# A hybrid S5 / gated-MLP layer: two loads moved to other queues, products with x's low half put last, one stage of the state-space mixer issued a block later

## The chip, the cores and the metric

The kernel runs on one core of a Trainium2 chip. Its engines work side by side, each through a queue of its own: TensorE (PE in the profile, PEld for its weight loads) multiplies, VectorE (DVE), ScalarE (ACT) and GpSimd (POOL) work element by element, and DMA transfers are issued from the queues of SyncE (SP), ScalarE or GpSimd. An engine waits only for the semaphores of its own next instruction. The metric is the device time of one execution in microseconds (us). Less is better.

## The reference

One layer on x of 256 tokens by 2048 columns, all in float32:

```
h   = rmsnorm(x, norm_mix_g)
z   = h @ w_in                          # 2048 -> 3072: [ssm_in 1024 | sgu_u 1024 | sgu_v 1024]
a   = s5(ssm_in), then y * sigmoid(y @ glu_w + glu_b) with y = gelu(s5 output)
b   = gelu(u) * (causal mixing of layernorm(gelu(v)) inside chunks of 128 + bias)
x   = x + concat(rmsnorm(a), rmsnorm(b)) @ w_out          # 2048 -> 2048
x   = x + relu(rmsnorm(x) @ w_up)^2 @ w_down              # 2048 -> 8192 -> 2048
out = rmsnorm(x, norm_final_g)
```

The S5 mixer has 64 groups of 16 channels with 64 complex states each, a diagonal recurrence over the 256 tokens.

## The kernel before

**Two halves for every operand.** A float32 product is made from rounded halves: `split` (line 110) writes the high half with ScalarE and the remainder with VectorE. A product is the sum of three: high weight by high activation, high weight by low activation, low weight by high activation (`which` = 0, 1, 2 in `block_A`). Weights stream through `wparts` (lines 149 to 187): a load of 512 KB on SP's queue brings a pair of row blocks (`raw`, four buffers), and `split` turns it into `whi` and `wlo` (three buffers each).

**Blocks.** `block_A` (line 189) makes 512 output columns with the weights stationary; its activations are `xT`, the transposed x, in a high and a low half. `block_B` (line 242) has the activations stationary and 512 weight columns moving: for each pair, two token halves by two row blocks by three products, 12 in all. The input projection for S5 is two `block_A`s of eight pairs each (lines 798 to 804). Then come the other input projections (`block_B` and `block_A`), the first half of the output projection `wout_half(8, ...)` (four `block_B`s n = 0 to 3 of four pairs, line 988), the GLU (`block_A` with `yhl`, line 1003), the second half of the output projection and the MLP.

**The first block.** x arrives in column blocks of 256 during the first block. `load_x(0)` (line 286) loads the first ones, one token half from SP's queue and one from ScalarE's; the norm's scale `gnat` comes from GpSimd's queue (line 287). `prep_x(i)` (line 347) transposes a column block on TensorE, then ScalarE writes the high half of `xT` with the scale (line 361) and VectorE the low half (line 362). `mids` is a list of seven calls of `prep_x`; a pair of the first block takes one of them in its middle, so that the columns for the next pair are made while this pair is multiplied. The first pair has its own order already (lines 202 to 211); the others take a call after `m == 1`, that is, after 12 of their 24 products.

**Background work.** The S5 mixer is written as generators in the list `bg`; each `yield` names a cost. `pump(d)` (line 117) adds d to a debt and issues pieces until the debt is paid; the blocks call it between their products. `gen_rest` runs the four rounds r = 0 to 3: `gen_f` (states from inputs), `gen_rot` (the recurrence), `gen_lane` (tables for later rounds; with `gen_k` the copies into `Tp` at line 693) and `gen_y` (line 754: 8 products with `Tp`, 16 with `Gp`, which a TensorE profile shows as 16 and 32 passes; then a GELU into `yst`, eight stores to `yd`, and the load of `yT`). `gen_y(r)` runs in round r + 1, and `gen_y(3)` is the last thing in `gen_rest`. The low and high half of `yT` are read by the GLU. `fence(last)` and `behind()` make the next four products of a block stand behind `last` in TensorE's queue. `tc.issue_after(ins)` puts instructions behind another one in the same engine's queue.

The order of each engine's queue is fixed before the run by a scheduler that goes by priority and by what is ready in its own model of time.

Of the kernel before, what the change touches and what calls it, by code (L numbers as in the profile page):

```python
# [18 lines left out]
P = 128  # L19
# [31 lines left out]
def hybrid_layer_kernel(  # L51
# [6 lines left out]
    nc = tc.nc  # L58
    V, A, T, G = nc.vector, nc.scalar, nc.tensor, nc.gpsimd
# [29 lines left out]
    def acc(shape, name="acc"):  # L89

        acc_pools.append(acc_pools.pop(0))
        return acc_pools[-1].tile(shape, F32, tag="acc", name=nm(name))
# [4 lines left out]
    def sx(shape, name="sx"):  # L97
        return pss_.tile(shape, F32, tag="sx", name=nm(name))

    def sq2k(shape, tag, bufs, name=None):  # L100
        return sp.tile(shape, F32, tag=tag, bufs=bufs, name=nm(name or tag))
# [11 lines left out]
    bg = []  # L113
# [3 lines left out]
    def pump(d):  # L117

        debt[0] += d
        while bg and debt[0] > 0:  # L120
            try:
                with tc.high_priority(offset=0):
                    c = next(bg[0])
                debt[0] -= c[0] + 0.4 * c[1] + 1 * c[2]
            except StopIteration:
                bg.pop(0)

    def drain_bg():
        while bg:
            pump(1e9)  # L130
# [3 lines left out]
    def fence(ins):  # L134

        fences[:] = [ins.ins] * 4

    def behind():
        return tc.issue_after(fences.pop()) if fences else nullcontext()


    KS = 2
    stream = {"pool": wp1, "fine": True, "kd": 2, "raw": 4, "d": 0.0}
# [3 lines left out]
    mids = []  # L147
# [41 lines left out]
    def block_A(w, k0, nk, c0, act):  # L189


        banks = [acc([P, 2, S], "accA") for _ in range(2)]
        def product(m, kk, which, kp, hi, lo):
            wt = (hi, hi, lo)[which][:, kk, m * P : m * P + P]
            return T.matmul(  # L195
                banks[m // 2][:, m % 2], wt, act(kp)[which == 1],
                start=(kp == 0 and m % 2 == 0 and which == 0), stop=(kp == nk - 1 and which == 2),
                skip_group_check=True,
            )

        for kp0, hi, lo in wparts(w, k0, nk, c0):
            if kp0 == 0 and len(mids) == 7:

                for kk in range(KS):
                    for which in (0, 2, 1):
                        for m in range(4):
                            last = product(m, kk, which, kk, hi, lo)
                    if kk == 0:
                        mids.pop(0)(last)
                pump(stream["d"])  # L210
                continue
            for m in range(4):
                for kk in range(KS):
                    for which in range(3):
                        with behind() if which == 0 else nullcontext():
                            last = product(m, kk, which, kp0 + kk, hi, lo)
                stream["last"] = last
                if m == 1 and mids:
                    mids.pop(0)(last)
                pump(stream["d"] / 4)  # L220
        return banks
# [40 lines left out]
    gnat = const.tile([16, P], F32, name="gnat")  # L262
# [5 lines left out]
    def load_x(c, engines=(nc.sync, nc.sync)):  # L268
        cs_ = slice(c, c + 256)
        for t in range(2):  # L270
            engines[t].dma_start(xin[t][:, cs_], x[t * P : (t + 1) * P, cs_])
# [11 lines left out]
                nc.sync.dma_start(vnat[r0 : r0 + n, :], v[0].rearrange("(k p) -> k p", p=P))  # L283
            r0 += n

    load_x(0, (nc.sync, nc.scalar))
    nc.gpsimd.dma_start(gnat, norm_mix_g[0].rearrange("(k p) -> k p", p=P))


    ident = const.tile([P, P], F32, name="ident")  # L290
# [120 lines left out]
    Tp = sp.tile([P, RP, 2, 4, 16], F32, name="Tp")  # L411
# [289 lines left out]
    u2, yTs = {}, {}  # L701
# [20 lines left out]
    def gen_f(r):  # L722
        pfs[r] = [sx(sh, "pf") for _ in range(2)]
        for q in range(RP):
            for i in range(2):
                T.matmul(pfs[r][i][:, q], w1s[r][:, i, q], u2[r][:, q], start=True, stop=True)  # L726
            yield 0.0, 0.0, 0.45

    def gen_rot(r):
        cosT, sinT, rhoT = tabs[r]  # L730
        h = [sq2k(sh, "hc", 2) for _ in range(2)]
        yield from cmul(h, cosT, sinT, pfs[r][0], pfs[r][1], sh, ALU.add, ALU.subtract)
        fl = "p q c -> p (q c)"
        for i in range(2):
            V.tensor_tensor_scan(
                h[i].rearrange(fl), rhoT.rearrange(fl), h[i].rearrange(fl), 0.0, ALU.mult, ALU.add
            )
            yield 0.6, 0.0, 0.0

        for i in range(2):  # L740
            t1, t2 = tmp([P, RP, NC4 - 1]), tmp([P, RP, NC4 - 1])
            V.tensor_tensor(t1, h[i][:, :, e63], cosT[:, :, e63], ALU.mult)
            yield 0.6, 0.0, 0.0
            V.tensor_tensor(t2, h[1 - i][:, :, e63], sinT[:, :, e63], ALU.mult)
            yield 0.6, 0.0, 0.0
            for g in range(2):
                gs_ = slice(g * 64, (g + 1) * 64)
                V.tensor_tensor(
                    Eg[i * 64 : (i + 1) * 64, :, g, 1:], t1[gs_], t2[gs_],
                    ALU.subtract if i == 0 else ALU.add,  # L750
                )
                yield 0.6, 0.0, 0.0

    def gen_y(r):
        py = sx(sh, "py")

        for q in range(RP):
            T.matmul(  # L758
                py[:, q], Tp[:, q].rearrange("p g j c -> p (g j c)"), u2[r][:, q],
                start=(q == 0), stop=False, skip_group_check=True,  # L760
            )
            if q % 2 == 1:
                yield 0.0, 0.0, 0.45
        for g in range(2):
            for q in range(RP):
                last = T.matmul(  # L766
                    py[g * 64 : (g + 1) * 64, q], Gp[:, q, g].rearrange("p j c -> p (j c)"), Eg[:, q, g],
                    start=False, stop=True, skip_group_check=True,
                )
        fence(last)  # L770
        yield 0.0, 0.0, 1.6
        yst = sq2k(sh, "zst", 2, "yst")
        A.activation(yst, py, AF.Gelu_apprx_tanh)
        rows_ = yd[r * 256 : (r + 1) * 256]
        for g in range(2):
            for j in range(4):
                p0 = g * 64 + j * 16
                nc.sync.dma_start(
                    rows_[:, j, :].rearrange("(q g p) c -> g p q c", g=2, p=16)[g], yst[p0 : p0 + 16]
                )  # L780
        yTs[r] = sq2k([P, 2, 4, NC4], "uy", 5, "yT")
        nc.sync.dma_start(yTs[r], rows_.rearrange("(m p) j c -> p m j c", p=P))
        yield 0.0, 0.5, 0.0

    def zip_gens(*gens):
        gens = list(gens)
        while gens:
            for g_ in list(gens):
                try:
                    yield next(g_)  # L790
                except StopIteration:
                    gens.remove(g_)
# [5 lines left out]
    for n in range(2):  # L798
        banks = block_A(w_in, 0, 16, n * 512, act_xT)
        with tc.high_priority(offset=AHEAD):  # L800
            if n == 0:
                x_rstd()
            for i, bank in enumerate(banks):
                z_out(n * 2 + i, bank)
# [14 lines left out]
    def gen_out_lane(r):  # L819

        if r > 0:
            yield from gen_y(r - 1)
        yield from gen_lane(r)

    def gen_rest():
        yield from gen_f(0)
        for r in range(4):
            yield from zip_gens(gen_rot(r), gen_out_lane(r))
            if r < 3:
                yield from gen_f(r + 1)  # L830
        yield from gen_y(3)

    bg.append(gen_rest())
    stream["d"] = PACE

# [20 lines left out]
    for n in range(2):  # L856
# [5 lines left out]
        if n == 1:  # L862
# [15 lines left out]
            for side in range(2):  # L878
                for i, half in enumerate(halves[side]):
                    if half is not None:  # L880
                        which = 0 if side == 0 else (1 if i < 3 else 2)
# [25 lines left out]
    def bhl(h):  # L907
        return bfirst[h // 2][:, h % 2] if h < 4 else hls[0][:, 1, h]
# [60 lines left out]
    rsb = const.tile([P, 2], F32, name="rsb")  # L969
# [10 lines left out]
    def wout_half(kt0, act, rs):  # L980
        for n in range(4):
            banks = block_B(w_out, kt0, 8, n * 512, act)
            for t in range(2):
                sl = x2[t][:, n * 512 : (n + 1) * 512]
                V.scalar_tensor_tensor(sl, banks[t], rs[:, t : t + 1], sl, ALU.mult, ALU.add)
            yield n

    for _ in wout_half(8, lambda k: (bhl(k)[:, 0], bhl(k)[:, 1]), rsb):
        pass
    drain_bg()  # L990
    stream["d"] = 0.0

# [9 lines left out]
    for n in range(2):  # L1002
        banks = block_A(glu_w, 0, 8, n * 512, lambda k: (yhl[:, k, 0], yhl[:, k, 1]))
        for i in range(2):
            gt = tmpm([P, 2, 4, NC4], F32, "gt")
            for mm in range(2):
                m = n * 4 + i * 2 + mm
# [6 lines left out]
            for mm in range(2):  # L1014
                m = n * 4 + i * 2 + mm
# [22 lines left out]
    for n in wout_half(0, lambda k: (ahl[k // 4][:, k % 4, 0], ahl[k // 4][:, k % 4, 1]), rsa):  # L1038
# [3 lines left out]
        for k2 in range(2):  # L1042
            pt = sx([P, 2, S], "ptx2")
            for kk in range(2):
                k = n * 4 + k2 * 2 + kk
                for t in range(2):
                    T.transpose(pt[:, kk, t * P : (t + 1) * P], x2[t][:, k * P : (k + 1) * P], ident)
            for kk in range(2):
                k = n * 4 + k2 * 2 + kk
# [148 lines left out]
```

## Time and profile before

| | |
|---|---|
| three runs | 1046.34, 1048.33 (median), 1049.29 us |
| profiled execution | 1048.05 us, span 1046.2 us |
| TensorE busy | 1033.5 us, 99% |
| VectorE busy | 674.3 us, 64% |
| ScalarE busy | 551.1 us, 53% |
| GpSimd busy | 9.3 us, 1% |
| mean granted clock of TensorE | 0.992 |

The span is the time from the first to the last profiled event of one execution. Busy shares are means over stages with different limits, and matmuls are pipelined, so that a busy TensorE is not one at its peak. A granted clock of 1.00 is 2.4 GHz, 0.50 is 1.2 GHz. A few per cent of the matmul records can be missing.

### The profile page before, as it was taken

What the parts mean: (1) busy time and instruction counts of PE and PEld (TensorE: products, weight loads), DVE (VectorE), ACT (ScalarE), POOL (GpSimd) and SP (SyncE); (2) the same over time, 40 slices, a digit from 0 to 9 for tenths busy, and PEclk for the clock granted to TensorE, in tenths of its full rate; (3) what the DMA queues carried; (4) which work ended last, traced back from release to release, by engine and by line L of the source; (5) the groups of instructions that cost most, each with busy time, mean ns of one, the idle gap of its engine ahead of it and who ended that gap; (6) DMA issues with size and microseconds to landing.
All of it is one profiled execution on the core that took longest, in us unless ns stands there. A gap on an engine that the chain in (4) does not pass through costs nothing.

```text
span 1046.2 us, 15091 instructions
## 1 busy us (share of the span) xinstructions
PE 1033.5 (99%) x5865; PEld 896.6 (86%) x5865; DVE 674.3 (64%) x957; ACT 551.1 (53%) x748; POOL 9.3 (1%) x23
## 2 busy tenths in 40 slices
PE   9999999999999999999999999999999999999996
PEld 8998899978988888888888888888888888888886
DVE  7998998765687665544466655456665565655564
ACT  5677658653766555544445543445554334545452
POOL 0100010000000000000000000000000000000000
PEclk9999999989999999999999999999999999999998
DMA  8964555546565666666666666666656566665662
GB/s 280 249 196 129 143 164 159 156 112 214 183 221 161 203 191 190 193 189 199 188 194 186 193 188 196 191 195 183 187 189 191 194 194 191 187 196 185 197 218 85
DMA packets 113047, 195.13 MB, mean 187 GB/s; under 512 B 17864, under 2 KB 23440, under 8 KB 112528
## 3 DMA queue, kind: packets, MB, share of 16 engines
q1 hardware_dynamic: 112112, 193.34, 60.8%
q8 instruction: 46, 0.75, 0.3%
q10 hardware_dynamic: 576, 0.79, 0.2%
q14 instruction: 25, 0.20, 0.1%
q0 software_dynamic: 288, 0.04, 0.0%
HBM read 189.91 MB, written 4.19 MB: 186 GB/s over the span
## 4 chain that ended last, share of the span: by engine, by line
PE 95%; DMA 2%; ACT 1%; DVE 1%; SPq 0%; issue 0%; DVEq 0%
PE accA L235 23%; PE accB L252 15%; PE accB L253 15%; PE accB L254 14%; PE accA L236 11%; PE accA L195 9%; PE pf L726 1%; DMA xin<-in_x_dram 1%; PE py L766 1%; PE py L758 1%; PE accL L1144 1%; PE accL L1143 1%; PE accL L1142 1%; PE pw L621 1%; PE pk L675 1%; PE pm L922 0%
## 5 line engine op out<-in xcount | busy, mean ns | idle before, releaser
L110 DVE TENSOR_TENSOR wlo<-raw,whi 128x1024 fp32r<-128x1024 f32 (+1 forms) x337 | 411.2, 1221 | 329.7 <-ACT whi L110 329.2
L110 ACT ACTIVATE whi<-raw 128x1024 fp32r<-128x1024 f32 (+1 forms) x337 | 356.1, 1059 | 401.3 <-PE accB L254 200.7
L235 PE MATMUL accA<-x2T,whi 128*128 128x512 f32 x1024 | 355.4, 395 | 0.0
L236 PE MATMUL accA<-x2T,wlo 128*128 128x256 f32 x1024 | 280.3, 278 | 0.0
L235 PEld LDWEIGHTS accA<-x2T,whi 128*128 128x128 f32 x1024 | 191.6, 188 | 43.6
L236 PEld LDWEIGHTS accA<-x2T,wlo 128*128 128x128 f32 x1024 | 192.6, 188 | 1.8
L254 PE MATMUL accB<-whi,hT 128*128 128x512 f32 x480 | 186.8, 389 | 0.0
L253 PE MATMUL accB<-wlo,hT 128*128 128x512 f32 x480 | 186.7, 389 | 0.0
L252 PE MATMUL accB<-whi,hT 128*128 128x512 f32 x480 | 167.9, 389 | 0.0
L254 PEld LDWEIGHTS accB<-whi,hT 128*128 128x128 f32 x480 | 90.1, 188 | 18.7
L253 PEld LDWEIGHTS accB<-wlo,hT 128*128 128x128 f32 x480 | 90.1, 188 | 18.6
L252 PEld LDWEIGHTS accB<-whi,hT 128*128 128x128 f32 x480 | 90.0, 188 | 18.6
L195 PE MATMUL accA<-xT,whi 128*128 128x256 f32 x512 | 101.1, 293 | 1.1 <-DVE xT L362 1.1
L195 PEld LDWEIGHTS accA<-xT,whi 128*128 128x128 f32 x512 | 80.2, 191 | 3.1 <-DVE xT L362 2.1
L195 PE MATMUL accA<-xT,wlo 128*128 128x256 f32 x256 | 71.5, 287 | 0.0
L195 PEld LDWEIGHTS accA<-xT,wlo 128*128 128x128 f32 x256 | 48.1, 191 | 0.0
L1096 ACT ACTIVATE cr<-accA 128x256 f32<-128x256 f32 x64 | 24.0, 374 | 7.9 <-PE accA L236 7.9
L253 PE MATMUL accB<-wlo,xT 128*128 128x512 f32 x64 | 25.9, 405 | 0.0
L254 PE MATMUL accB<-whi,xT 128*128 128x512 f32 x64 | 25.2, 394 | 0.0
L252 PE MATMUL accB<-whi,xT 128*128 128x512 f32 x64 | 24.9, 407 | 0.0
L254 PE MATMUL accB<-whi,ahl 128*128 128x512 f32 x64 | 24.8, 393 | 0.0
L253 PE MATMUL accB<-wlo,ahl 128*128 128x512 f32 x64 | 24.8, 393 | 0.0
(291 smaller groups left out, 1026.2 us busy)
## 6 DMA issues: line engine op xcount, KB each, us to landing
raw<-in_w_up_dram SPq DMA_DIRECT2D x128, 512.0 KB, 3.7
raw<-in_w_down_dram SPq DMA_DIRECT2D x128, 512.0 KB, 4.4
raw<-in_w_in_dram SPq DMA_DIRECT2D x47, 512.0 KB, 4.3
raw<-in_w_out_dram SPq DMA_DIRECT2D x32, 512.0 KB, 4.7
raw<-in_ssm_glu_w_dram SPq DMA_DIRECT2D x8, 512.0 KB, 4.3
x<-in_x_dram SPq DMA_DIRECT2D x2, 1024.0 KB, 7.2
xin<-in_x_dram SPq DMA_DIRECT2D x15, 128.0 KB, 4.8
out_dram<-dacc SPq DMA_DIRECT2D x5, 256.0 KB, 4.0
```

Source lines behind the costliest of these rows:

```text
L110: return A.activation(hi, src, AF.Copy), V.tensor_sub(lo, src, hi.bitcast(F32))
L195: return T.matmul(banks[m // 2][:, m % 2], wt, act(kp)[which == 1], start=(kp == 0 and m % 2 == 0 and which == 0), stop=(kp == nk - 1 and ...
L235: T.matmul(o, hi[:, kk, ms], xhl, start=(kp == 0), stop=False, skip_group_check=True)
L236: T.matmul(o[:, 1], lo[:, kk, ms], xhl[:, 0], start=False, stop=(kp == nk - 1), skip_group_check=True,)
L252: T.matmul(banks[t], xh[:, ts_], hi[:, kk], start=(kp == 0), stop=False)
L253: T.matmul(banks[t], xh[:, ts_], lo[:, kk], start=False, stop=False)
L254: stream["last"] = T.matmul(banks[t], xl[:, ts_], hi[:, kk], start=False, stop=(kp == nk - 1))
L621: T.transpose(pw[:, k], Qb[:, i, h2 * 4 + k].rearrange("p e g h -> p (e g h)"), ident)
L675: last = T.matmul(pk[:, q].rearrange("p d c -> p (d c)"), Qb[:, i, q, 0].rearrange("p g h -> p (g h)"), gcs[r][i][:, q, 0:4].rearrange("p ...
L726: T.matmul(pfs[r][i][:, q], w1s[r][:, i, q], u2[r][:, q], start=True, stop=True)
L758: T.matmul(py[:, q], Tp[:, q].rearrange("p g j c -> p (g j c)"), u2[r][:, q], start=(q == 0), stop=False, skip_group_check=True,)
L1096: A.activation(cr[:, mm], b_[:, 1], AF.Copy)
```

## The change

Three things are edited. The first x columns are both loaded from SP's queue, and the norm's scale from ScalarE's. In the first block, the pairs that still have a `prep_x` to place issue the 16 products with the high half of x first, place `prep_x` after the eighth, and issue the eight products with the low half last, calling `pump` there. `gen_y(3)` is taken out of `gen_rest`; after block n = 0 of the output projection's first half the background list is emptied, then `gen_y(3)` is appended to it, and its first products stand behind the last product issued so far.

```diff
@@ block_A @@
                 pump(stream["d"])
                 continue
+            if mids:
+                for kk in range(KS):
+                    for m in range(4):
+                        for which in (0, 2):
+                            last = product(m, kk, which, kp0 + kk, hi, lo)
+                        if kk == 0 and m == 3:
+                            mids.pop(0)(last)
+                for m in range(4):
+                    for kk in range(KS):
+                        last = product(m, kk, 1, kp0 + kk, hi, lo)
+                    stream["last"] = last
+                    pump(stream["d"] / 4)
+                continue
             for m in range(4):
...
-    load_x(0, (nc.sync, nc.scalar))
-    nc.gpsimd.dma_start(gnat, norm_mix_g[0].rearrange("(k p) -> k p", p=P))
+    load_x(0)
+    nc.scalar.dma_start(gnat, norm_mix_g[0].rearrange("(k p) -> k p", p=P))
...
@@ gen_y @@
         for q in range(RP):
-            T.matmul(
-                py[:, q], Tp[:, q].rearrange("p g j c -> p (g j c)"), u2[r][:, q],
-                start=(q == 0), stop=False, skip_group_check=True,
-            )
+            with tc.issue_after(stream["last"].ins) if r == 3 else nullcontext():
+                T.matmul(
+                    py[:, q], Tp[:, q].rearrange("p g j c -> p (g j c)"), u2[r][:, q],
+                    start=(q == 0), stop=False, skip_group_check=True,
+                )
...
@@ gen_rest @@
             if r < 3:
                 yield from gen_f(r + 1)
-        yield from gen_y(3)
...
-    for _ in wout_half(8, lambda k: (bhl(k)[:, 0], bhl(k)[:, 1]), rsb):
-        pass
+    for n in wout_half(8, lambda k: (bhl(k)[:, 0], bhl(k)[:, 1]), rsb):
+        if n == 0:
+            drain_bg()
+            bg.append(gen_y(3))
     drain_bg()
```

## Rows read from the trace of the kernel before

**Rows 1.** The page, busy us, share and instructions of each engine.
```profile
PE 1033.5 (99%) x5865; PEld 896.6 (86%) x5865; DVE 674.3 (64%) x957; ACT 551.1 (53%) x748; POOL 9.3 (1%) x23
```
**Rows 2.** Waits: us in total, times, longest; the third of the first 36 us.
```profile
PE py L758 <- ACT Tp L693: 2.1, 1, 2.1
...
PE accA L195 <- DVE xT L362: 1.1, 4, 0.4
...
PEld accA L195 <- DVE xT L362: 2.1, 5, 0.6
```
**Rows 3.** Windows: length, busy us of PE, PEld, DVE, ACT, POOL, PEclk, DMA, GB/s.
```profile
0.00:35.00 35.00, 32.76 (x242) 31.17 (x243) 28.77 (x99) 22.71 (x45) 1.68 (x9) 1.00 0.90 261
...
213.40:220.90 7.50, 7.50 (x52) 7.17 (x52) 6.65 (x13) 4.84 (x8) 0.00 (x0) 0.53 0.25 72
220.90:224.10 3.20, 3.20 (x10) 2.49 (x9) 1.54 (x10) 0.60 (x1) 0.00 (x0) 0.50 0.27 35
224.10:240.00 15.90, 15.90 (x71) 13.08 (x70) 9.28 (x10) 6.54 (x7) 0.00 (x0) 1.00 0.65 191
```
**Rows 4.** Timeline of TensorE, output projection: start, us, what, [idle before <-releaser].
```profile
213.39 3.25 PE L758 MATMUL py<-u,Tp 128*128 128x64 f32 x16 [2.12 <-ACT Tp L693]
...
220.94 0.80 PE L252 MATMUL accB<-whi,hl 128*128 128x512 f32 x1
...
227.98 0.40 PE L252 MATMUL accB<-whi,bfirst 128*128 128x512 f32 x1
...
238.97 0.64 PE L252 MATMUL accB<-whi,bfirst 128*128 128x512 f32 x2
```
**Rows 5.** Timeline of ScalarE in the same stretch.
```profile
209.02 4.32 ACT L693 ACTIVATE Tp<-k,gmask 32x128 f32<-32x128 f32 x8
...
214.70 1.04 ACT L110 ACTIVATE whi<-raw 128x1024 fp32r<-128x1024 f32 x1
```
**Rows 6.** Timeline of VectorE in the same stretch.
```profile
207.56 1.22 DVE L110 TENSOR_TENSOR wlo<-raw,whi 128x1024 fp32r<-128x1024 f32 x1
...
209.50 0.86 DVE L930 SCALAR_TENSOR_TENSOR hl<-uT,vecs,hl 128x256 fp32r<-128x256 f32 x2
...
215.89 1.22 DVE L110 TENSOR_TENSOR wlo<-raw,whi 128x1024 fp32r<-128x1024 f32 x1
...
218.83 1.21 DVE L110 TENSOR_TENSOR wlo<-raw,whi 128x1024 fp32r<-128x1024 f32 x1
```
**Rows 7.** Timeline of TensorE, the second products of an earlier `gen_y`.
```profile
113.54 1.90 PE L766 MATMUL py<-Eg,Gp 128*64 128x64 f32 x32
```
**Rows 8.** Timelines of the first block: VectorE, TensorE's weight loads, TensorE.
```profile
12.85 1.23 DVE L110 TENSOR_TENSOR wlo<-raw,whi 128x1024 fp32r<-128x1024 f32 x1 [1.55 <-ACT whi L110]
...
14.53 0.19 PEld L195 LDWEIGHTS accA<-xT,whi 128*128 128x128 f32 x1 [0.21 <-DVE xT L362]
...
31.06 0.60 PE L355 MATMUL ptx<-ident,xin 128*128 128x128 f32 x4
...
33.24 0.38 PE L195 MATMUL accA<-xT,whi 128*128 128x256 f32 x1 [0.39 <-DVE xT L362]
```
**Rows 9.** Timeline of all engines at the start; ACTq and SPq issue transfers.
```profile
0.80 0.41 ACTq L271 DMA_DIRECT2D xin<-in_x_dram  x1
0.80 0.39 SPq L271 DMA_DIRECT2D xin<-in_x_dram  x1
...
1.24 0.90 SPq L159 DMA_DIRECT2D raw<-in_w_in_dram  x2
...
1.34 0.63 POOL L287 DMA_DIRECT2D gnat<-in_norm_mix_g_dram  x1 [0.84 <-POOLq L1184]
```
**Rows 10.** Timeline of SP's queue; DMA issues with KB each and us to landing.
```profile
221.67 3.68 SPq L778 DMA_DIRECT2D yd<-yst  x8
...
raw<-in_w_out_dram SPq DMA_DIRECT2D x32, 512.0 KB, 4.7
...
yd<-yst SPq DMA_DIRECT2D x32, 32.0 KB, 1.8
```

## Prediction, made before the changed kernel was run

> **What bounds the kernel now.** I read the page's busy table first: TensorE has work in 99% of the span [rows 1], so the time is its own work plus the few places where it stands still or runs slowly, and only a change to those can move the end. The list of its waits names those places [rows 2]: one wait of 2.1 us, in front of the products of `gen_y` with `Tp`, released by ScalarE's copies into `Tp`; and four, 1.1 us together, in the first block, released by VectorE writing x's low half. The weight loads in front of the same products wait longer, 2.1 us in five places; loads run ahead of their products, so the block loses between 1.1 and 2.1 us. Last I cut the stretch around the long wait into windows [rows 3]. The wait is the smaller part of the loss: after it the granted clock is 0.53 for 7.5 us and 0.50 for 3.2 us, the lower of the two levels (1.2 GHz), and it is 1.00 again in the next window. At full clock these 10.7 us would be 7.5 x 0.47 + 3.2 x 0.50 = 5.1 us shorter. Wait and slow clock cost 7.2 us together.
>
> **The moved `gen_y(3)`.** Names: the first half of the output projection has blocks n = 0 to 3, each with four pairs of weight rows, each pair with 12 wide products. The wait stands after the second pair of n = 0, at 213.39 - 2.12 = 211.27 us [rows 4]. TensorE's order there is: `gen_y(3)`, pair 3, pair 4, then n = 1 from 227.98 and n = 2 from 238.97. The 48 products of n = 1 give a step of 10.99 / 48 = 0.229 us.
>
> With the change bg is drained after n = 0, so the debt stands above zero when `gen_y(3)` is appended, and the first `pump` of n = 1 issues all of it, behind the first three products of n = 1. What does TensorE find at 211.27 instead? Pair 3 is ready: its low weights are done at 207.56 + 1.22 = 208.78, its activations at 209.50 + 0.86 = 210.36 [rows 6]. Twelve products take 2.75 us, to 214.02. Pair 4 isn't: ScalarE is busy with the eight `Tp` copies from 209.02 to 213.34, then with `hl`, and its high weights follow at 214.70 + 1.04 = 215.74 [rows 5]; VectorE's low weights are done at 215.89 + 1.22 = 217.11 [rows 6]. Neither depends on `gen_y`, so I leave both where they are. So TensorE waits 1.7 us, can do at most two products with high weights (0.46 us, to 216.20), waits 0.9 us more to 217.11, and has ten left: 2.3 us, to 219.4. What was hidden under `gen_y(3)` becomes the new wait: the same ScalarE queue, one step later. The four small passes for the statistics fit into that second wait and are counted at nothing; without it they come on top.
>
> In n = 1 the first product runs at 219.4, the second needs low weights that are done at 218.83 + 1.21 = 220.04 [rows 6]: 0.4 us. Then `gen_y(3)`. Its inputs have been ready since 213.34, so it costs passes alone: 32 passes of the second kind took 1.90 us at full clock [rows 7]; the 16 of the first kind, 3.25 us at the low clock [rows 4], are an estimated 1.6 to 1.7: 3.6 us. The block ends at 219.4 + 0.4 + 3.6 + 48 x 0.229 = 234.4, against 238.97: 4.6 us gained if the clock holds.
>
> Does it? Before, 2.12 us of waiting dropped it; small passes, busy throughout, did not raise it in 7.5 us, while 3.2 us of wide products behind them did [rows 3]. After, 2.6 us of waiting stand in two pieces around two products, followed at once by wide products. Lower bound: no fall, nothing. Upper bound: a fall as long as today's, 5.1 us. The nearest row is the 3.2 us of wide products: half of it is lost, 1.6 us. I take 1.5: 3.1 us gained.
>
> What is late next? Queued behind the later `gen_y(3)` are ScalarE's `yst`, eight stores to `yd` on SP's queue, the load of `yT`, and the last split for the GLU. That split is wanted only after n = 3, two whole blocks (22 us) after n = 1: hidden. The stores hold SP up, a rival below. The fence now holds four products of n = 1 instead of n = 0, behind passes whose inputs are ready: nothing.
>
> **The first block.** In six of its eight pairs the 16 products with x's high half come first, the eight with the low half last, and the transposes for the next columns go out after eight products instead of twelve. A product is moved, none is added, and each loads its weights as before. Today the second product of a pair wants the low half. In the last pair it came 33.24 - 31.06 = 2.18 us after the transposes began [rows 8]. A step here is 0.12 us (256 columns against 512 for 0.229 us), so four products earlier is 0.5 us more head start, which covers that wait of 0.39 us; in the six pairs the low half is wanted 16 products, 1.9 us, later still. So the four waits go. The price: low weights are now wanted second instead of third, 0.12 us sooner. In the third pair they are done at 12.85 + 1.23 = 14.08, with the weight load waiting until 14.53 for x [rows 8]: 0.45 us of room, and not more, when that wait goes. `pump` moves to the pair's end, with the same debt; the small VectorE work it issues is spread less evenly, at no cost that a row shows. Bounds: -2.1 us (all weight-load waits) and +0.7 (no wait saved, one step of 0.12 lost in each of six pairs). I take -1.2.
>
> **The start.** The second x load leaves ScalarE's queue at 0.80 us and follows the first on SP; two SP issues took 0.90 us together [rows 9], so this load and everything behind it on SP, all first weights included, goes 0.45 us later. The scale leaves POOL, whose issue started at 1.34 and took 0.63, for ScalarE's queue at 0.80: about 0.5 us earlier at least, and it frees POOL for the identity. The first product needs the scale, the x columns and weights. Bounds +0.45 and -0.5; I take 0. The Trainium skill, "DMA: Bandwidth & Descriptors", section "Issuing engines are not separate DMA queues", speaks against this edit: starting transfers from several engines saves only the issuing time, so joining two on one queue gives that time away. The two rows at 0.80 us on ScalarE's queue and on SP [rows 9] agree with it; by the rule alone the edit is +0.45 us in place of 0.
>
> **Sum.** The profiled execution took 1048.05 us (a span of 1046.2 and 1.85 around it, which stays; 0.28 below the median of the runs, which range over 2.95). 1048.05 - 3.1 - 1.2 + 0 = 1043.75; I say 1043.8.
>
> **Rivals.**
> A, the forecast: a shorter wait in a new place, a short fall of the clock: 1043.8, own range 1042.6 to 1045.5. Chance 0.42.
> B, same waits, but the clock holds, since the waiting is cut in two: 1048.05 - 4.6 - 1.2 = 1042.2. For it: four waits of up to 0.39 us in the first block left the clock at 1.00 [rows 3]. Against: 2.6 us is more than 2.12. Chance 0.22.
> C, the clock falls late enough that `gen_y(3)`'s small passes, which did not raise it before, keep it down as long as today: 1042.2 + 5.1 = 1047.3. Chance 0.14.
> D, no new wait: ScalarE's order changes so that pair 4's weights go ahead of the `Tp` copies, which nobody then hurries for. 27.7 us (211.27 to 238.97) become 72 x 0.229 + 3.6 = 20.1: 1048.05 - 7.6 - 1.2 = 1039.3. Against: nothing in the diff touches that order. Chance 0.08.
> E, the other side: SP stands behind the stores of `yst`. They were issued from 221.67 for 3.68 us [rows 10]. Now `yst` is done about 224.8; the stores end at 228.5 and land 1.8 us later; if the weights of n = 2 stand behind them and the `yT` load that waits for them, they go out about 230.3, land 4.7 us later [rows 10], and are split (1.04 + 1.22) at 237.3, against 234.4: 2.9 us of waiting and a second fall of 1.6 to 5.1 us: 1043.8 + 4.5 to 1043.8 + 8.0, so 1048.3 to 1051.8. It decides if those weights are issued after 234.4 - 4.7 - 2.3 = 227.4. Against: their buffers come free at about 220, before the stores can go. Chance 0.07.
> F, the front does not do what it says: the loads 0.45 us later put the third pair's low weights at 14.53, where the wait ended before, and the later pairs gain only what the start lost: 1048.05 - 3.1 + 0.45 = 1045.4. Chance 0.07; the rule named above is on its side.
>
> **Numbers.** About 0.3%, 3.1 us, is what a measurement of this kernel tells from no change; against the median, faster means under 1045.2 and slower over 1051.5. Faster: 0.35 of A, B, D: 0.65. Same: 0.07 of A, C, F, and 0.02 of E: 0.30. Slower: the rest of E, 0.05. The range leaves out D and most of E: 1040.8 to 1047.4.
>
> **What would show it.** TensorE's wait for `Tp` is gone; in its place stands a wait for the split weights of pair 4 of n = 0, in two pieces near 1.7 and 0.9 us; `gen_y(3)` runs in n = 1 in about 3.6 us at clock 1.00; a low-clock window is absent or near 3 us. In the first block no wait for x's low half remains, one for low weights may. The prediction is wrong if ScalarE's queue there is ordered otherwise, if the low clock lasts 10 us again, or if SP's weights stand behind the stores.

## The result, and the profile of the changed kernel

The changed kernel takes 1042.59 us (median of 6 runs, 1042.48 to 1043.27), the kernel before 1048.02 (6 runs, 1046.34 to 1049.29): a ratio of 0.9949, 95% interval 0.9938 to 0.9960, faster by more than 0.3%. The forecast was 1043.8, range 1040.8 to 1047.4. The profiled execution took 1042.58 us, with a span of 1040.8; the one before had 1046.2 [rows 3, 4 are of it].

Lines behind 211 have numbers 14 to 16 higher than before. First the page's table of busy times, then the list of TensorE's waits (us in total, times, longest):

```profile
PE 1028.0 (99%) x5865; PEld 891.9 (86%) x5865; DVE 672.9 (65%) x957; ACT 551.6 (53%) x748; POOL 9.3 (1%) x22
```
```profile
PE accB L266 <- ACT whi L110: 1.8, 1, 1.8
...
PE accA L195 <- DVE xT L376: 0.6, 1, 0.6
PE accB L267 <- DVE wlo L110: 0.6, 2, 0.3
PE accA L195 <- DVE wlo L110: 0.4, 1, 0.4
```

As many instructions, and TensorE is busy for 5.5 us less: the time was not taken out of the waits alone. The wait for `Tp` [rows 2] is gone; the longest is now one for the split weights (`whi`). The windows of the output projection's beginning (columns as in rows 3) show what happened to the clock:

```profile
204.00:214.00 10.00, 8.77 (x42) 6.86 (x40) 6.94 (x13) 8.57 (x17) 0.00 (x0) 1.00 0.45 138
214.00:219.50 5.50, 4.36 (x19) 3.33 (x20) 5.47 (x11) 4.93 (x7) 0.00 (x0) 1.00 0.29 98
219.50:224.00 4.50, 4.50 (x53) 4.23 (x52) 4.19 (x14) 0.70 (x2) 0.00 (x0) 1.00 0.75 245
224.00:240.00 16.00, 16.00 (x71) 13.13 (x70) 8.40 (x9) 6.59 (x7) 0.00 (x0) 1.00 0.67 195
```

The granted clock is 1.00 throughout, where it was 0.53 and 0.50 for 10.7 us [rows 3]. TensorE's timeline of the stage, first one more row of the kernel before, then the rows of the changed kernel that answer to rows 4:

```profile
205.48 0.51 PE L252 MATMUL accB<-whi,bfirst 128*128 128x512 f32 x1
```
```profile
204.26 0.51 PE L266 MATMUL accB<-whi,bfirst 128*128 128x512 f32 x1
...
214.56 0.73 PE L266 MATMUL accB<-whi,hl 128*128 128x512 f32 x2 [1.79 <-ACT whi L110]
215.13 0.50 PE L980 MATMUL pssb<-onesm,sqt 128*128 128x1 f32 x4
215.94 0.50 PE L267 MATMUL accB<-wlo,hl 128*128 128x512 f32 x1 [0.30 <-DVE wlo L110]
...
219.01 0.50 PE L267 MATMUL accB<-wlo,bfirst 128*128 128x512 f32 x1 [0.27 <-DVE wlo L110]
...
219.58 1.89 PE L774 MATMUL py<-u,Tp 128*128 128x64 f32 x16
221.40 1.90 PE L782 MATMUL py<-Eg,Gp 128*64 128x64 f32 x32
...
233.60 0.64 PE L266 MATMUL accB<-whi,bfirst 128*128 128x512 f32 x2
```

n = 0 begins 1.2 us sooner than before and n = 2 begins 5.4 us sooner (238.97 [rows 4]); behind that nothing changes: the rest takes 807.2 us in both (the span less the start of n = 2). So the gain is 1.2 us in front of n = 0 and 4.15 us between the starts of n = 0 and n = 2, called the stage below. ScalarE's rows answer to rows 5: the eight `Tp` copies still stand ahead of the weights' split that the wait is for.

```profile
207.79 4.32 ACT L707 ACTIVATE Tp<-k,gmask 32x128 f32<-32x128 f32 x8
212.13 0.91 ACT L944 ACTIVATE hl<-uT,vecs 128x256 fp32r<-128x256 f32 x2
...
213.47 1.04 ACT L110 ACTIVATE whi<-raw 128x1024 fp32r<-128x1024 f32 x1
```

In the front, TensorE's timeline has its first product 0.24 us later than before (7.00), a new wait of 0.35 us for the second pair's low weights, and the last pair's wait for x's low half, which in rows 8 stood at 33.24. VectorE's row says why: it makes that low half behind two splits of weights.

```profile
7.24 0.73 PE L195 MATMUL accA<-xT,whi 128*128 128x256 f32 x4
...
11.38 0.39 PE L195 MATMUL accA<-xT,wlo 128*128 128x256 f32 x1 [0.35 <-DVE wlo L110]
...
32.64 0.38 PE L195 MATMUL accA<-xT,whi 128*128 128x256 f32 x1 [0.61 <-DVE xT L376]
```
```profile
29.57 1.21 DVE L110 TENSOR_TENSOR wlo<-raw,whi 128x1024 fp32r<-128x1024 f32 x1
...
30.98 1.21 DVE L110 TENSOR_TENSOR wlo<-raw,whi 128x1024 fp32r<-128x1024 f32 x1
32.12 0.47 DVE L376 SCALAR_TENSOR_TENSOR xT<-ptx,vecs,xT 128x256 fp32r<-128x256 f32 x1
```

The same product comes 0.60 us sooner. The other 0.6 us of the front arise in the second block: its transposes `pc` and the two products for `prs` took turns before, from 46.40 to 48.2, and now stand in groups. The kernel before, then the changed kernel:

```profile
46.40 0.40 PE L553 MATMUL pc<-ident,bcn 64*128 64x64 f32 x3
46.73 0.49 PE L384 MATMUL prs<-dg,onesm 128*128 128x128 f32 x2
...
47.35 0.49 PE L384 MATMUL prs<-dg,onesm 128*128 128x128 f32 x2
```
```profile
44.86 0.60 PE L398 MATMUL prs<-dg,onesm 128*128 128x128 f32 x4
46.23 0.71 PE L567 MATMUL pc<-ident,bcn 64*128 64x64 f32 x8
```

### The profile page after: what moved, and what is told of

Its sections match the earlier page's. It is cut to its first block, busy times and chain, and to the rows that moved or that the text cites. A ratio compares the mean times of both kernels' runs of the same rounds, so it can differ in the third digit from the quotient of the medians.

```text
span 1040.8 us, 15088 instructions
## 1 busy us (share of the span) xinstructions
PE 1028.0 (99%) x5865; PEld 891.9 (86%) x5865; DVE 672.9 (65%) x957; ACT 551.6 (53%) x748; POOL 9.3 (1%) x22
## 4 chain that ended last, share of the span: by engine, by line
PE 94%; DMA 2%; ACT 2%; DVE 1%; SPq 0%; issue 0%; DVEq 0%
PE accA L249 23%; PE accB L266 14%; PE accB L267 14%; PE accB L268 14%; PE accA L250 11%; PE accA L195 9%; PE pf L740 1%; DMA xin<-in_x_dram 1%; PE accL L1161 1%; PE accL L1159 1%; PE accL L1160 1%; PE pw L635 1%; PE py L782 1%; PE py L774 1%; PE pk L689 1%; DVE wlo L110 0%
```

## The experiments

My theory after the result: the stage's 4.15 us are a fall of the clock that no longer comes, and the new wait is the old ScalarE queue one step later. The rivals: the stage's order itself is shorter, or the front gains more than its 1.2 us. All times of one group of runs share the runs of the kernel before on the same chip.

### Each part alone

`gen_y(3)` alone:
```diff
+            with tc.issue_after(stream["last"].ins) if r == 3 else nullcontext():
                 T.matmul(py[:, q], ...)
-        yield from gen_y(3)
-    for _ in wout_half(8, ...): pass
+    for n in wout_half(8, ...):
+        if n == 0:
+            drain_bg()
+            bg.append(gen_y(3))
```

> The kernel before with the third edit alone: gen_y(3) issued in block n = 1, loads and first block as before. Theory (the moved stage brings most of it, since the wait in front of the split weights is shorter than the one for Tp and the clock holds): 4.1 to 4.3 us under the kernel before, near 1043.8. Rival (front and stage share it about equally, the stage gains less when it is reached 1.2 us later): 2.5 to 3 us under it. In its trace n = 2 of the output projection should start 4.1 us earlier than 238.97, and the wait for Tp should be replaced by one of 1.8 us for the high weights.

Measured: 1045.54 us (10 runs, 1044.41 to 1047.06), ratio 0.9996 (0.9987 to 1.0006). The wait is the one expected (1.79 us, for the high weights), but n = 2 starts only 2.8 us sooner, at 236.16, and neither reading's time came.

The first block's order alone, the `if mids:` part of the diff:

> The kernel before with the new order of products in the first block alone; loads as before. Theory (the order gains what the loads do not lose): with the low weights of the second pair 0.4 us sooner than after, 1.3 to 1.7 us under the kernel before. Rival (the gain at the front came from the order of the small transposes in the second block, by chance): 0.6 us under it or less.

Measured: 1043.78 us (10 runs, 1042.04 to 1045.40), ratio 0.9973 (0.9963 to 0.9983), more than either reading allowed.

The two loads alone (`load_x(0)`, and `nc.scalar` for the scale):

> The kernel before with the two loads moved to other queues alone. Theory (one SP issue more ahead of the first weights): the first product of the first block 0.24 us later, the whole 0.2 to 0.5 us over the kernel before. Rival (the scale's earlier arrival pays): 0 to 0.3 us under it.

Measured: 1047.88 us (10 runs, 1045.28 to 1048.96), ratio 1.0007 (0.9995 to 1.0020): no difference clear of the noise.

That was not what I had expected: the part that was to bring most brings nothing clear of the noise alone (the medians differ by 1.2 us, but the interval of the ratio holds 1), and the one that was to bring 1.2 us brings 2.8. The windows of the stages (length, busy TensorE, clock, DMA share, GB/s) show that the clock fell in both, for a short time. First with `gen_y(3)` alone, then with the block's order alone:

```profile
217.60:221.10 3.50, 3.50 (x9) 0.51 0.45 150
```
```profile
214.30:217.80 3.50, 3.50 (x34) 0.51 0.12 40
```

With the block's order alone the `Tp` wait is where it was (2.1 us, small passes behind it), and yet the clock is low for 3.4 us, not for 10.2. So the length of the fall is no property of the place.

### The kernel before, once more

> The kernel before, unchanged, for a second profile of it and for what two series of one kernel differ by. The stage is taken from the first product of n=0 to the first of n=2: 33.49 us in the kernel before with the clock low for 10.24 us; 30.25 with the block order alone and 30.35 with the moved gen_y(3) alone, both with 3.41 us low; 29.34 in the changed kernel with no fall. Theory (moving gen_y(3) gains by the clock alone, its waits being as long in the new place): the stage's length goes by the low time alone, 29.4 without a fall, 30.3 for 3.4 us, about 31.8 for 6.8, 33.5 for 10.2. Rival (the old place costs time of its own): at the same low time the stage is over 1 us longer than those. The two series of times differ by under 0.3%.

Measured: 1046.69 us (10 runs, 1044.39 to 1049.13), against 1047.16 for the kernel before beside it; ratio 0.9992 (0.9979 to 1.0005). The same kernel, the same wait in front of the same passes, and another fall. TensorE's timeline, then the windows of the stage (length, busy TensorE, clock, DMA share, GB/s):

```profile
206.08 0.51 PE L252 MATMUL accB<-whi,bfirst 128*128 128x512 f32 x1
...
213.99 2.56 PE L758 MATMUL py<-u,Tp 128*128 128x64 f32 x16 [2.12 <-ACT Tp L693]
216.47 2.51 PE L766 MATMUL py<-Eg,Gp 128*64 128x64 f32 x26
...
237.49 0.64 PE L252 MATMUL accB<-whi,bfirst 128*128 128x512 f32 x2
```
```profile
206.08:215.20 9.12, 7.00 (x37) 1.00 0.49 150
215.20:218.70 3.50, 3.50 (x32) 0.51 0.00 0
218.70:237.49 18.79, 18.26 (x87) 1.00 0.59 176
```

The profiled executions side by side (us; each row from that kernel's timeline and windows). The time at low clock is worked out from the windows' means: 3.50 us at 0.51 are 3.4 us at 0.50 and the rest at 1.00; of the loads alone, 11.0 us have a mean of 0.53, some 10.3 us at 0.50.

| kernel | first product | n = 0 | stage | clock low for | behind it | span |
|---|---|---|---|---|---|---|
| before [rows 3, 4] | 7.00 | 205.48 | 33.49 | 10.2 | 807.2 | 1046.2 |
| before, again | 7.36 | 206.08 | 31.41 | 3.4 | 807.3 | 1044.8 |
| loads alone | 7.15 | 206.02 | 33.51 | 10.3 | 807.2 | 1046.7 |
| `gen_y(3)` alone | 7.17 | 205.81 | 30.35 | 3.4 | 807.2 | 1043.4 |
| block's order alone | 7.18 | 204.49 | 30.25 | 3.4 | 807.3 | 1042.0 |
| changed | 7.24 | 204.26 | 29.34 | none | 807.2 | 1040.8 |

Read at one length of the fall, 3.4 us, the stage is 1.1 us shorter with the moved `gen_y(3)` and 1.2 with the block's order alone, so the rival holds by its number: at the same low time the kernel before takes over 1 us longer. But its reason, the old place, is not shown: with the block's order alone `gen_y(3)` stands in the old place, behind the same wait, and the stage is as short. What the second profile of the kernel before has and these two have not is a wait of 0.53 us for low weights in n = 1, at 232.33; with the block's order alone the four passes for the statistics also stand among wide products and not inside `gen_y(3)`, because the scheduler orders that stage anew. What makes the other 0.5 us stays open.

The clock is the rest. `gen_y(3)` alone and the changed kernel have the same order of the stage and the same wait of 1.79 us: 30.35 to 29.34 is 1.0 us for 3.4 us at the low level. From 31.41 to 33.49 it is 2.1 us for 6.8 us more, although the longer one has no wait in n = 1. The changed kernel's 4.15 us are therefore 2.1 of a long fall that the kernel before doesn't always have, 1.0 of a short one, and 1.1 of the order and its wait. On top of the block's new order, moving `gen_y(3)` shortens nothing at an equal fall (30.25 and 30.35); the lower median there, 1042.59 against 1043.78, comes with fewer falls (see the mean clocks below).

All the executions of the kernel before, in the four groups of experiments, say the same with more numbers. The 28 with a mean granted clock of 0.998, which is that of the changed kernel's profile without a fall, took 1044.39 to 1046.26 us, 1045.4 on average; the 20 with 0.992, that of the profile with the long fall, 1047.69 to 1049.13, 1048.5 on average. Four of the changed kernel's six executions have 0.998 and took 1042.48 to 1042.59; the other two, with 0.997 and 0.996, 1043.27 and 1043.25; of the ten with the block's order alone none has more than 0.997. So without a fall on either side some 2.8 us of the 5.4 are left, and the changed kernel may still fall in some executions. The kernel before of the first result, with 1048.02, was also slower than in the later groups, whose medians are 1046.69 to 1047.23.

### Is the new wait ScalarE's queue?

First the `Tp` copies were only placed later in the program, behind n = 0, with `gen_y(3)` behind n = 1:

> The changed kernel with the eight Tp copies of the last round taken out of ScalarE's way: they are issued in block n = 1, and gen_y(3) in n = 2. Theory (the wait of 1.8 + 0.3 + 0.3 us in front of the split weights is ScalarE's time in those copies, moved on): the waits go, 2.2 to 2.6 us under the changed kernel, near 1040.2. Rival (the split weights come late for another reason, their load or VectorE): under 0.5 us gained.

Measured: 1042.84 us (7 runs, 1042.66 to 1043.73), ratio 0.9967 (0.9955 to 0.9978), wait 2.0 us. The scheduler put the copies where they had been, at 207.92, ahead of the split: the edit did not do what it was for and says nothing about the theory. It does show that `gen_y(3)` in n = 2 instead of n = 1 gains nothing by itself. So an edge was added:

```diff
-                        split(hi, lo, raw[:, s : s + KS])
+                        stream["split"] = split(hi, lo, raw[:, s : s + KS])
...
+                with tc.issue_after(stream["split"][0].ins) if r == 3 else nullcontext():
                     A.activation(Tp[...], k4[...], AF.Copy, scale=gmask[:, g : g + 1])
...
+        if n == 0:
+            drain_bg()
+            bg.append(gen_tp(3))
+        if n == 1:
+            drain_bg()
+            bg.append(gen_y(3))
```

> The changed kernel, with the eight Tp copies of stage 3 held on ScalarE until the split of n=0's last weight pair has been issued, so that the second pair of hl and that split come some 4.3 us earlier, and with gen_y(3) moved from n=1 to n=2. Theory (the remaining waits in n=0, 1.8 + 0.3 + 0.3 us, are ScalarE's 4.3 us of Tp copies ahead of the split): all three go, the first product of n=1 comes 2.4 us sooner, the granted clock never falls, median 1040.2 (1039.8 to 1040.8). Rival (the split is next limited by something else, the weights' landing or the gate's products): the wait at pair 4 stays over 1 us with another releaser, median 1041.5 to 1042.8.

Measured: 1040.64 us (4 runs, 1040.53 to 1041.57), ratio to the kernel before 0.9940 (0.9921 to 0.9958). ScalarE's timeline: the split that was wanted ends at 210.60 instead of 214.51, and the copies stand behind it and the next one. TensorE has one wait left there:

```profile
209.55 1.05 ACT L110 ACTIVATE whi<-raw 128x1024 fp32r<-128x1024 f32 x1
...
213.01 4.56 ACT L716 ACTIVATE Tp<-k,gmask 32x128 f32<-32x128 f32 x8
```
```profile
219.96 0.50 PE L267 MATMUL accB<-wlo,bfirst 128*128 128x512 f32 x1 [0.53 <-DVE wlo L110]
```

The 1.8 us are gone, and the clock is 1.00 through the stage. The gain over the changed kernel, which was measured in another group of runs, is 1.95 us by the medians and 2.0 by the spans (1040.8 to 1038.8), instead of 2.4: the copies now hold up the next split, hence the 0.53. The theory holds. This is the fastest kernel of the study.

### What sets the length of the fall?

The `Tp` copies of stage 3 were made a second time (`for x_ in range(8 if r == 3 else 0): A.activation(Tp[...], ...)`), in the changed kernel and in the kernel before:

> The changed kernel, with stage 3's eight Tp copies made a second time on ScalarE (the same values once more, nothing left out). The wait at pair 4 of n=0 grows by 4.3 us, to about 6 us, and is followed by products of 512 columns. Theory (what follows a wait sets how long the clock stays low): the clock falls in every execution, for about 3.4 us each time, mean granted clock 0.996 to 0.997; median 1042.6 + 4.3 + 1 = 1047.9 (1047 to 1049). Rival (the length of the fall goes by the idle time alone): low for 6.8 to 10.2 us, mean granted clock 0.992 to 0.995, median 1049 to 1050.

> The kernel before, with stage 3's eight Tp copies made a second time. Its wait for Tp grows from 2.1 to about 6.4 us and is followed by gen_y(3)'s passes of 64 columns. Theory (small passes after a wait keep the clock low): low for 10.2 us in every execution, mean granted clock 0.992 to 0.993, median 1045.5 (the kernel before where its clock holds) + 4.3 + 3 = 1052.8 (1052 to 1054). Rival (what follows makes no difference): the same spread of mean clocks as with the copies doubled in the changed kernel, median near 1050.5.

Measured: 1046.09 us (10 runs, 1045.64 to 1049.93) and 1054.36 us (4 runs, 1053.77 to 1054.63). TensorE's waits in the stage of the first, then of the second, and one window of the second:

```profile
215.06 0.74 PE L266 MATMUL accB<-whi,hl 128*128 128x512 f32 x2 [2.44 <-ACT whi L110]
...
222.14 0.50 PE L267 MATMUL accB<-wlo,bfirst 128*128 128x512 f32 x1 [0.76 <-DVE wlo L110]
```
```profile
216.87 1.01 PE L972 MATMUL pssb<-onesm,sqt 128*128 128x1 f32 x4 [4.42 <-DVE sqt L969]
...
221.65 3.67 PE L765 MATMUL py<-u,Tp 128*128 128x64 f32 x16 [3.78 <-ACT Tp L700]
```
```profile
214.00:227.90 13.90, 7.26 (x48) 0.55 0.23 77
```

The times fit neither expectation well: the first lies under both of its ranges, with two of ten runs at 1049.8 and 1049.9, and the second is 0.4 us over its range, with the clock low for longer than the 10.2 us expected. The direction fits the theory (3.4 us low in the first profile, 12.5 of the 13.9 us in the second), but the pair doesn't test it: the scheduler put six of the eight repeated copies of the first kernel behind the split that TensorE waits for, so that its waits (2.44, 0.60 and 0.76) grew by 1.4 us in all, not by 4.3, while the second waits 8.2 us. What sets the length of a fall stays open.

### The start

```diff
-    load_x(0)
+    load_x(0, (nc.sync, nc.scalar))
     nc.scalar.dma_start(gnat, ...)
```

> The changed kernel, with the second half of x back on ScalarE's queue and the norm's scale behind it on that queue. The changed kernel's first product stands at 7.24 us, the kernel before's at 7.00, and a weight that lands late brings a new wait of 0.4 us at 11.4 us. Theory (two x loads on SP's queue cost that delay): first product near 7.0, the wait at 11.4 us gone, median 1042.1 (1041.8 to 1042.4). Rival (the first product's place differs from execution to execution, and the queues make no difference): 1042.6 within 0.3, with first products between 7.0 and 7.25.

Measured: 1044.44 us (8 runs, 1042.57 to 1046.05). The scale was issued first all the same (0.79 us on ScalarE's queue, x at 1.23). TensorE's timeline; then a row of the changed kernel; then the kernel with the copies made twice, which starts with the changed kernel's loads:

```profile
4.58 0.61 PE L347 MATMUL pwarm<-onesm 128*128 128x128 f32 x4
...
6.25 0.74 PE L195 MATMUL accA<-xT,whi 128*128 128x256 f32 x4
...
10.72 0.39 PE L195 MATMUL accA<-xT,wlo 128*128 128x256 f32 x1 [0.40 <-DVE wlo L110]
```
```profile
5.12 1.06 PE L347 MATMUL pwarm<-onesm 128*128 128x128 f32 x4
```
```profile
4.75 0.61 PE L347 MATMUL pwarm<-onesm 128*128 128x128 f32 x4
...
6.35 0.74 PE L195 MATMUL accA<-xT,whi 128*128 128x256 f32 x4
```

The first product comes 1.0 us sooner than in the changed kernel's profile, but the queues are not shown to be the cause. TensorE doesn't wait there: from 1.11 us on it works through 24 warm-up products (`pwarm`) with the first transposes among them, and four of these took 1.06 us in the changed kernel's profile and 0.61 here. In the third profile, with both x loads on SP, they took 0.61 as well, and the first product stands at 6.35. Over all profiles it stands at 6.35 to 7.36 with both loads on SP (seven) and at 7.00 to 7.37 with the old loads (six). What does come later with both loads on SP is the split of the second pair's weights: it starts at 8.57 to 9.54 us in those seven profiles, at 8.20 in the kernel before and at 8.35 here.

n = 0 comes 0.75 us later than in the changed kernel (205.01): the first 46 us have 0.5 us more of waits for low weights and 0.5 us of a new one for x's high half. In the stage the clock fell for 3.4 us. The fastest run, 1042.57, equals those of the changed kernel. The theory fell: the wait behind the first products is still there, and nothing was gained. Of the rival, the differing place of the first product holds, its time doesn't.

### The last pair, and the second block's order

The first block's last pair, too, low half last (its condition becomes `if mids or kp0 == nk - KS` for that block):

> The changed kernel, with the first block's last pair taken low half of x last as well. In the changed kernel its first low product still waits 0.61 us at 32.64, because VectorE makes two splits of weights ahead of that low half (they end at 32.19). Theory: sixteen products without the low half last some 1.9 us, from 31.8 to 33.7, and the low halves are there at 32.6 and 33.3, so the wait goes whole: median 1042.0 (1041.7 to 1042.3). Rival (the wait turns up at the next weights, whose split ends later): 1042.6 within 0.3, with another wait of 0.3 to 0.6 us between 31 and 36.

Measured: 1045.67 us (10 runs, 1044.87 to 1046.15): 3 us slower than the changed kernel (of another group of runs; the spans are 1044.3 and 1040.8). The wait at 32.64 is gone, as the theory said; the `pc` transposes that began at 43.13 begin at 42.76. But n = 0 begins at 206.27, 2.0 us later. Between 44 and 204 us TensorE waited for nothing in the changed kernel; here it waits twice:

```profile
85.92 0.73 PE L269 MATMUL accB<-whi,xT 128*128 128x512 f32 x2 [0.67 <-ACT whi L110]
...
133.81 0.65 PE L885 MATMUL pwt<-ident,wbuf 128*128 128x128 f32 x4 [1.11 <-ACT lngw L886]
```

ScalarE's order there is another: the eight `Tp` copies run at 80.20 and the split behind them comes at 84.81, where the changed kernel has them at 76.62 and 82.51. The scheduler laid out all later work afresh around a front that was 0.4 us shorter. The stage is longer too: it has a wait of 1.68 us for the statistics and a fall of the clock.

The kernel before, with the third group of `pc` held behind `prs`:
```diff
-            T.matmul(prs_[:, t * P : (t + 1) * P], ...)
+            stream["prs"] = T.matmul(prs_[:, t * P : (t + 1) * P], ...)
...
-                with tc.issue_after(stream["last"].ins):
+                with tc.issue_after((stream["prs"] if which == 1 else stream["last"]).ins):
```

> The kernel before, with one edge added: the third group of pc transposes in the second block comes behind both prs products. In the kernel before, prs, pc and prs take turns on TensorE at 46.4 to 48.2; in the changed kernel they stand in groups, and its second block ends some 0.6 us earlier against its first block's end. Theory (taking turns between small transposes and prs costs that 0.6 us, and the new block order brought it along by chance of the order): the first product of n=0 comes 0.6 us sooner after the first block's end, median 0.6 us under the kernel before on the same chip. Rival (the 0.6 us come from the new block order itself, from weights and low halves that are ahead): the distance from the first block's last product to n=0 is unchanged within 0.2, and the median too within 0.5.

Measured: 1047.92 us (10 runs, 1047.56 to 1049.20), ratio 1.0013 (1.0003 to 1.0022). From the last pair's first low product to n = 0 it is 171.86 us (33.14 to 205.00), against 172.24 in the kernel before and 172.23 in its second profile: 0.38 us less, and that with a new wait of 0.65 us for low weights at 132.95 in between. So the taking of turns can account for all of the 0.6 us; the new wait keeps the sum from being exact. The time shows none of it, for the stage was reordered too, and TensorE waits twice there instead of once:

```profile
212.86 0.61 PE L965 MATMUL pssb<-onesm,sqt 128*128 128x1 f32 x4 [2.06 <-DVE sqt L962]
215.15 3.68 PE L758 MATMUL py<-u,Tp 128*128 128x64 f32 x16 [1.69 <-ACT Tp L693]
```

The held copies and the last pair together:

> The changed kernel with the held Tp copies and with the last pair of the first block low half last, both. Theory (the two sit in different places and add up): 1040.6 less 0.6, median 1040.0 (1039.6 to 1040.4), no wait over 0.6 us left on TensorE between 7 us and 500 us. Rival (what is taken off the front comes back in the stage, where the weights' landing then ends last): 1040.6 within 0.3.

Measured: 1041.57 us (6 runs, 1041.10 to 1041.94), 0.9 us slower than the held copies alone by the medians, 1.2 by the spans: n = 0 begins at 206.16, behind the same two waits, of 0.7 and 1.1 us. Neither reading: the front's gain was lost before the stage, not in it.

## Why the prediction was right, and where it was not

**The stage: the mechanism was right.** The wait moved behind the same ScalarE queue, in two pieces of 1.79 and, with the statistics' passes in between, 0.30 us (forecast 1.7 and 0.9 with the passes in the second), and 0.27 in n = 1 (forecast 0.4). `gen_y(3)` took 3.65 us (219.58 to 223.23; forecast 3.6), at full clock. From n = 0 to n = 2 it is 29.34 us, against 28.92 by the sum (234.4 less 205.48): n = 1's low weights came 0.2 us later, and the products around the waits and the steps of 0.230 us make the rest.

**The clock's term was mis-sized.** I took 1.5 us for a short fall; in the profile there was none, and that term, less the stage's 0.4 us, makes up nearly all of the miss of 1.2 us (1043.8 to 1042.59). Why there was none is not shown: with `gen_y(3)` alone the clock fell behind the same wait in the same order. Of the forecast's cases, the price of B (1042.2) is the nearest to the measured 1042.59. The deeper flaw is in the term of 4.6 us: it took the fall in the one profile that I had as part of the kernel. The second profile of the same kernel has 3.4 us of low clock instead of 10.2 and a span 1.4 us shorter. There the clock is back at 1.00 at 218.70, while `gen_y(3)`'s passes run on to 219.9, so the reading that small passes did not raise it (also rival C's) was a reading of one profile. Moving `gen_y(3)` is worth 1.1 us at an equal fall against the second profile (31.41 to 30.35), half of it a wait in n = 1; what comes on top comes only against executions with a longer fall. That is why it is worth nothing measurable by itself: its own executions fall too. That the forecast lies so near owes something to luck: it started from a profile with the long fall, and the kernel before that it was measured against was just as slow (1048.02).

**The first block: the right sum from the wrong terms.** Forecast -1.2, measured -1.22 against the first profile (205.48 to 204.26) and -1.82 against the second (206.08). But the step "so the four waits go" failed: three went, the last pair's stayed at 0.61 us, because the half microsecond of head start meets a VectorE queue with two splits of 1.21 us ahead, and a wait for low weights came at 11.38. The block itself gave 0.60 us (1.21 against the second profile), the second block 0.6, through an order of small products that no step of mine contained; holding that order by itself gave 0.38 in spite of a new wait. Nor did I see that the new order changes the stage: by itself it brings 2.8 us, 1.6 in front of n = 0 and 1.2 in the stage (both against the second profile, at the same fall).

**The start: right in the sum, not in its terms.** 0 was forecast, and the loads alone gave a ratio of 1.0007 (0.9995 to 1.0020). But neither +0.45 nor -0.5 is seen at the first product: TensorE is at its warm-up products and transposes until then, without a wait for x or the scale, and how long these take differs by 1 us from profile to profile. The Trainium skill's rule ("DMA: Bandwidth & Descriptors", section "Issuing engines are not separate DMA queues"), that a second issuing engine saves only issuing time, would have made it 0.45 us slower. The trace agrees as far as the issuing goes: SP issues the first weights at 1.71 us instead of 1.24 [rows 9]. In the time no run shows it.

**The rivals.** C and E did not occur: SP issued the weights first and the eight stores from 223.96 for 3.65 us, and nothing waited for what stood behind them. D, a ScalarE order with the split ahead of the copies, is what the added edge made: forecast 1039.3, measured 1040.64. F occurred in small, one pair earlier, as the wait of 0.35 us at 11.38; the front gained all the same.

## What to carry to other kernels

A stall that appears after a step is moved out of its way is often the same queue, one step later: another 1.95 us were to be had by ordering ScalarE's queue. Where an edit changes when things are ready, compare the order of instructions on every engine far behind it as well: here one saved wait of 0.6 us was followed by new waits of 0.67 and 1.11 us, 50 and 100 us later. And before a loss is put into a sum, profile the same kernel twice.

## What the runs showed of the hardware that was not expected

After the same wait of 2.12 us, in front of the same passes, TensorE's granted clock was 0.50 for about 10.2 us in one execution of the kernel before and for about 3.4 us in another. Behind a wait of 1.79 us it did not fall at all in the changed kernel's profile, and with `gen_y(3)` alone it fell behind the same wait. What decides it stays open. Such falls explain part of the spread of one kernel's times: of 10 runs of the kernel before, from 1044.39 to 1049.13, the three with a mean clock of 0.998 took 1045.1 on average, the two with 0.992, 1048.9. Low clock costs less than half its length: 1.0 us for 3.4 us where order and waits are the same, 2.1 us for 6.8 us more in the kernel before.
